# A two-layer attention kernel: the second layer's heads ordered by time, and the last head's row halves exchanged

## The chip, the cores and the metric

The kernel runs on one core of one Trainium2 chip. The metric is the device time of one execution in microseconds, the median of several runs; lower is better. The kernel before takes 1461.78 us (median of 3 runs, 1460.41 to 1463.3).

## The reference

A decoder trunk of two layers on an input of 1024 rows and 1024 columns, in float32. Layer A is differential attention with 8 heads; the change leaves its arithmetic and its order rule alone. Layer B is stick-breaking attention with 16 heads of 64 columns, on keys and values that are projected from layer A's output. Cut to what matters, layer B is

```python
k, v = split(rms(x, kv_norm) @ w_kv)
q, g = split(rms(x, b_norm) @ w_in)
for each head and each block of 128 rows i:
    z = (q_i @ k.T) / 8                          # columns 0 .. (i+1)*128
    log_1mb = where(mask, log_sigmoid(-z), 0)
    suffix = cumsum from the right of log_1mb, without the own column
    a = where(mask, exp(log_sigmoid(z) + suffix), 0)
    o_i = a @ v
x = x + (o * silu(g)) @ w_out
```

The causal mask makes the work of row block i (0 to 7) grow with i + 1: rows 512 to 1023 hold 26/36 of it, rows 0 to 511 hold 10/36.

## The kernel before, in words

Every float32 product is made of three float32r matmuls (high by high, low by high, high by low; two where the weights' low part is left out). Layer B works on 8 pairs of heads. For each pair there are four projections (k, v, q and the gate g), each in two halves of 512 rows, 24 matmuls of 128x512 each (`group`, L195 to L197). They don't depend on the attention of the pair before, and serve as **fill**: while TensorE works on a pair's attention it is given the next pair's projections in between. There are k tiles (`kh`, `kl`) for two pairs only.

The attention of a pair is cut into four **units** m = 0 to 3 of two row blocks, 2m and 2m + 1. A unit has two parts:

- S (`unit_s_b`): the scores of a block (`scores`, L237, one or two chunks of up to 512 columns, matmuls on 64 rows of the array, both heads side by side in PSUM tile `sc`, of which there is one), their copy by ScalarE (L781), the mask by GpSimd (L783), and then the chain: L790 (VectorE), L791 and L792 (ScalarE), L793 and the scan L795 (VectorE), L796 (ScalarE). Blocks 4 to 7 have a tile `zl` for each of the two heads; blocks 0 to 3 have one for both.
- T (`unit_t_b`): for each 256 columns of each head, transposes of the chain's result (`transposed`, L265, into PSUM tile `tr`), their split into `th` (ScalarE, L271) and `tl` (VectorE, L272), three buffers each, and the products with v (L811, L812).

`run_layer` sets the order in which these steps are written: S of one unit, T of the unit before, and so on, in the order 1, 3, 0, 2 (`ORDERS[2]`); `merge` mixes that list with the fill by estimated cost. The list is the order of priority. A scheduler that comes with the language then places each instruction on its engine's queue, and each engine runs its queue in that order.

The last pair has the output projection as its fill (`OutProj`). `last_order` is (1, 0, 3, 2) in the kernel before: the units of rows 0 to 511 first, mixed with the part of their output projection that needs heads 0 to 11 alone; then the units of rows 512 to 1023, mixed with the rest of the output projection of rows 0 to 511; and last, with nothing beside it, the output projection of rows 512 to 1023. The line that picks it is

```python
f0 = last_order[0] // 2
```

Of the kernel before, what the change touches and what calls it, by code (L numbers as in the profile page):

```python
# [19 lines left out]
P = 128  # L20
# [15 lines left out]
def build(tc, ins, out):  # L36
# [9 lines left out]
         "al": 6, "bl": 7, "tb": 3, "oa": 0, "la": 0, "lb": 8, "lt": 0, "lead": 1.0, "leada": 0.02, "leadb": 0.02, "leadxa": 0.15, "leadxb": 0.1, "holda": 0, "holdb": 0, "c2": 1, "gca": 0, "gcb": 0, "prea": 2, "preb": 1, "warm": 16, "wp": 2, "hpx": -1, "nx": 1, "nk": 6, "hpo": 0, "ob": 2, "late": 400}  # L46
# [37 lines left out]
    def zat(n):  # L84
        return zt()
# [97 lines left out]
    def group(n, pairs, done):  # L183
# [3 lines left out]
        size = 4 if n > 256 else 8  # L187
# [39 lines left out]
    def scores(q, k, i, evac):  # L227
# [3 lines left out]
        for off, w in reversed(chunks(n)):  # L231
# [7 lines left out]
            evac(off, w, n, pts)  # L239

# [33 lines left out]

    def v_rows(pt):
        vt = g2k()
        with hp():
            act.activation(vt, pt, AF.Copy)
        tr = PS("tr", B["tr"])
        for r in range(4):  # L280
            pe.transpose(tr[:, r * P:(r + 1) * P], vt[:, r * P:(r + 1) * P], ident)
        return tr


    def merge(main, fill, lead=0.0):
# [4 lines left out]
        while i < len(main) or j < len(fill):  # L290
# [4 lines left out]
            else:  # L295
                df += fill[j][0]
                fill[j][1]()
                j += 1

# [141 lines left out]
    def run_layer(hds, qkv, unit_s, unit_t, xT, og, op, hfs):  # L441
# [66 lines left out]
        for h in range(n - 1):  # L508
            main = []
# [12 lines left out]
        ss = unit_s(h, ma)  # L522
        main = (late + ss if B["lt"] else ss + late) + [(0.0, lambda: gate_mul(hds[h - 1], h - 1, og)),
# [72 lines left out]
    def unit_s_a(h, m):  # L596
        hd = heads_a[h]

        def s_step(qb):
            if hd.o is None:  # L600
                hd.o = [T("o", [P, HALF], B["o"]) for _ in range(2)]
                hd.at = {}
            n = (qb + 1) * P
            p = [zat(n + P), zat(n + P)]
            mn = [small(2), small(2)]

            def evac(off, w, n, pts):
                k = 0 if off == 0 else 1
                mask = mask_a[:, HALF - w:] if off + w == n else mask_a[:, 0:1].to_broadcast([P, w])
                for c in range(2):  # L610
                    dve.tensor_tensor_reduce(p[c][:, off:off + w], pts[:, c, :w], mask, 1.0, BIG, ALU.add, ALU.min,  # L611
                                             mn[c][:, k:k + 1])

            scores(hd.q[qb // 4], hd.k, qb, evac)
            s = small(2)
            for c in range(2):
                b = mn[c][:, 0:1]
                if n > 512:
                    dve.tensor_tensor(b, b, mn[c][:, 1:2], ALU.min)
                act.activation(p[c][:, :n], p[c][:, :n], AF.Exp, bias=b, scale=-1.0, accum_out=s[:, c:c + 1])  # L620
            r = small(2)
            dve.reciprocal(r, s)
            dve.tensor_tensor(r[:, 1:2], r[:, 1:2], nlam, ALU.mult)
            dve.tensor_scalar(p[0][:, :n], p[0][:, :n], r[:, 0:1], None, ALU.mult)
            dve.scalar_tensor_tensor(p[1][:, :n], p[1][:, :n], r[:, 1:2], p[0][:, :n], ALU.mult, ALU.add)
            hd.at[qb] = p[1]

        return [(4 * (qb + 1) * P * 0.42, lambda qb=qb: s_step(qb)) for qb in (2 * m, 2 * m + 1)]

    def unit_t_a(h, m):  # L630
# [3 lines left out]
        def t_step(t):  # L634
# [3 lines left out]
            for i, (kb, th, tl) in enumerate(transposed(hd.at[2 * m], hd.at[2 * m + 1], t, t == m)):  # L638
# [14 lines left out]
        return [(4 * 55 + 6 * 109 + (430 if t == m else 0), lambda t=t: t_step(t)) for t in range(m + 1)]  # L653
# [109 lines left out]
    def unit_s_b(p, m):  # L763
        hd = heads_b[p]

        def s_step(qb):
            if hd.o is None:
                hd.o = [T("o", [P, HALF], B["o"]) for _ in range(2)]
                hd.at = {}
            n = (qb + 1) * P  # L770
            heads = ((0, 1),) if n <= HALF else ((0,), (1,))
            z = [zbt() for _ in heads]
            w2 = len(heads[0]) * n
            for t in z:
                pool.memset(t[:, w2:w2 + 1], 0.0)
# [10 lines left out]
            scores(hd.q[qb // 4], hd.k, qb, evac)  # L786
            for t in z:
                zc = t[:, :w2]
                u = u4k()[:, :w2]
# [92 lines left out]
```

## Time and profile before

| | |
|---|---|
| median of 3 runs | 1461.78 us (1460.41 to 1463.3) |
| the profiled execution | 1463.71 us |
| its span, first to last instruction | 1461.8 us |
| mean granted clock | 0.985 |
| TensorE, matmuls busy | 1409.5 us, 96% |
| VectorE busy | 1073.2 us, 73% |
| ScalarE busy | 927.8 us, 63% |
| GpSimd busy | 294.9 us, 20% |

The busy share of TensorE is the union of its matmuls' spans. Matmuls overlap, so a long row of them is "busy" at any spacing; the idle time between them is a lower bound of what TensorE loses, and the spacing of their starts tells the rest. The first layer's attention runs from about 30 to 570 us, the change of layers to 755 us, the first seven pairs of layer B to 1297 us, the last pair to 1398 us, and what is left of the output projection to the end.

### The profile page before, as it was taken

The numbers are of one execution on the slowest core, as the hardware profiler recorded it, in microseconds if no ns is written. First come the engines' busy times: TensorE is split into PE (matmuls) and PEld (weight loads), VectorE is DVE, ScalarE is ACT, GpSimd is POOL, SyncE is SP. The second block draws the span as 40 slices with busy tenths as digits, with TensorE's granted clock in tenths as the row PEclk, the third lists the DMA queues.
The fourth block names the chain that finished last, engine by engine and source line by source line (L and its number), as shares of the span: only waits on it lengthen the run. The fifth ranks groups of instructions, "written<-read, shape, count | busy, mean of one in ns | idle before, by whom it ended". The sixth has DMA issues, their size and how long they took to land.

```text
span 1461.8 us, 24434 instructions
## 1 busy us (share of the span) xinstructions
PE 1409.5 (96%) x8944; PEld 1188.5 (81%) x8944; DVE 1073.2 (73%) x2219; ACT 927.8 (63%) x1908; POOL 294.9 (20%) x545
## 2 busy tenths in 40 slices
PE   8999999999999999999999999998999999987899
PEld 7888888888888888789877777776778677776699
DVE  7576667677777776775547888878878888888952
ACT  7555556566565655442557777778777877787720
POOL 0111212121212121100011222223233232335100
PEclk9999999999999999999999999999999999998999
DMA  5111111111111115621310011110011010233512
GB/s 203 59 30 44 45 44 44 44 44 44 44 44 44 44 61 185 214 90 58 116 58 29 30 58 29 44 44 30 34 45 38 30 58 30 70 133 111 193 73 80
DMA packets 43111, 99.39 MB, mean 68 GB/s; under 512 B 4848, under 2 KB 6640, under 8 KB 41968
## 3 DMA queue, kind: packets, MB, share of 16 engines
q1 hardware_dynamic: 42992, 97.83, 19.5%
q8 instruction: 71, 1.16, 0.3%
q14 instruction: 48, 0.39, 0.1%
HBM read 74.74 MB, written 23.07 MB: 67 GB/s over the span
## 4 chain that ended last, share of the span: by engine, by line
PE 75%; DVE 12%; ACT 6%; issue 4%; DMA 2%; POOL 1%; SPq 0%; DVEq 0%; POOLq 0%; ACTq 0%
PE proj L195 18%; PE proj L196 17%; PE proj L197 17%; PE sc L237 8%; PE tr L265 5%; DVE u4k L795 4%; DVE u4k L793 2%; DVE tl L272 2%; PE av L811 2%; PE av L812 2%; PE av L642 1%; ACT u4k L791 1%; PE av L640 1%; PE av L641 1%; ACT u4k L792 1%
## 5 line engine op out<-in xcount | busy, mean ns | idle before, releaser
L195 PE MATMUL proj<-ah,w 128*128 128x512 f32 x768 | 309.0, 402 | 5.4 <-DVE kl L245 5.3
L196 PE MATMUL proj<-al,w 128*128 128x512 f32 x768 | 308.5, 402 | 0.0
L197 PE MATMUL proj<-ah,w 128*128 128x512 f32 x768 | 306.4, 399 | 0.0
L195 PE MATMUL proj<-w,ah 128*128 128x256 f32 x992 | 291.2, 294 | 5.2 <-DVE kl L424 2.7
L197 PE MATMUL proj<-w,al 128*128 128x256 f32 x992 | 285.4, 288 | 0.0
L196 PE MATMUL proj<-w,ah 128*128 128x256 f32 x992 | 285.2, 288 | 0.0
L195 PEld LDWEIGHTS proj<-w,ah 128*128 128x128 f32 x992 | 192.3, 194 | 15.6 <-DVE kl L424 4.2
L197 PEld LDWEIGHTS proj<-w,al 128*128 128x128 f32 x992 | 192.3, 194 | 1.9 <-issue 1.6
L196 PEld LDWEIGHTS proj<-w,ah 128*128 128x128 f32 x992 | 192.3, 194 | 1.9 <-issue 1.3
L195 PEld LDWEIGHTS proj<-ah,w 128*128 128x128 f32 x768 | 145.6, 190 | 41.4 <-DVE kl L245 6.6
L795 DVE TENSOR_TENSOR_SCAN u4k<-zl,u4k 128x768 f32<-128x768 f32 (+4 forms) x96 | 173.7, 1812 | 1.0
L196 PEld LDWEIGHTS proj<-al,w 128*128 128x128 f32 x768 | 145.7, 190 | 33.0 <-issue 6.4
L197 PEld LDWEIGHTS proj<-ah,w 128*128 128x128 f32 x768 | 145.7, 190 | 32.1 <-issue 4.2
L237 PE MATMUL sc<-kh,q 64*128 64x512 f32 (+2 forms) x768 | 158.2, 400 | 12.6 <-ACT zl L781 9.8
L272 DVE TENSOR_TENSOR tl<-tr,th 128x512 fp32r<-128x512 f32 (+1 forms) x240 | 145.2, 629 | 32.5 <-ACT th L271 30.6
L783 POOL TENSOR_SCALAR_AFFINE_SELECT zl<-zl 128x128 f32<-128x128 f32 (+1 forms) x96 | 81.8, 857 | 306.3 <-ACT zl L781 298.5
L271 ACT ACTIVATE th<-tr 128x512 fp32r<-128x512 f32 (+1 forms) x240 | 124.4, 553 | 28.8 <-PE tr L265 24.5
L796 ACT ACTIVATE zl<-u4k 128x768 f32<-128x768 f32 (+4 forms) x96 | 81.3, 846 | 93.8 <-DVE u4k L795 81.2
L164 ACT ACTIVATE w<-raw,cols 128x256 fp32r<-128x256 f32 x240 | 104.6, 500 | 45.8 <-PE proj L196 33.5
L265 PE MATMUL tr<-ident,zl 128*128 128x128 f32 x864 | 129.0, 277 | 3.6 <-ACT zl L796 2.0
L611 DVE CUSTOM_DVE_ANT_0 zl<-sc,mask_a 128x384 f32<-128x384 f32 (+3 forms) x192 | 99.0, 552 | 40.7 <-PE sc L237 40.5
L237 PEld LDWEIGHTS sc<-kh,q 64*128 64x128 f32 x768 | 76.0, 187 | 64.6 <-issue 17.5
(146 smaller groups left out, 2590.9 us busy)
## 6 DMA issues: line engine op xcount, KB each, us to landing
raw<-in_w_kv_dram SPq DMA_DIRECT2D x32, 256.0 KB, 2.7
raw<-in_w_b_dram SPq DMA_DIRECT2D x32, 256.0 KB, 2.7
raw<-in_w_qk_dram SPq DMA_DIRECT2D x28, 256.0 KB, 2.7
raw<-in_w_vg_dram SPq DMA_DIRECT2D x28, 256.0 KB, 2.7
og_a<-o SPq DMA_DIRECT2D x28, 256.0 KB, 2.0
og_b<-o SPq DMA_DIRECT2D x28, 256.0 KB, 2.0
raw<-in_a_w_out_dram SPq DMA_DIRECT2D x26, 256.0 KB, 2.9
raw<-in_b_w_out_dram SPq DMA_DIRECT2D x26, 256.0 KB, 2.9
```

Source lines behind the costliest of these rows:

```text
L164: act.activation(h[:, i], r, AF.Copy, scale=g)
L195: pe.matmul(box["p"], lh, rh, start=(j == 0), stop=False)
L196: pe.matmul(box["p"], lh, rl, start=False, stop=False)
L197: pe.matmul(box["p"], ll, rh, start=False, stop=last)
L237: pe.matmul(pts[:, c, :wm], q[a][HI[c], rs_], k[b][HI[c], off:off + wm], start=(a + b == 0), stop=(a == 1))
L265: pe.transpose(pt[:, o:o + P], a[:, (2 * t + b) * P:(2 * t + b + 1) * P], ident)
L271: act.activation(th[:, skip:], pt[:, skip:], AF.Copy)
L272: dve.tensor_tensor(tl[:, skip:], pt[:, skip:], f32(th[:, skip:]), ALU.subtract)
L611: dve.tensor_tensor_reduce(p[c][:, off:off + w], pts[:, c, :w], mask, 1.0, BIG, ALU.add, ALU.min, mn[c][:, k:k + 1])
L783: pool.affine_select(t3[:, :, n - P:], t3[:, :, n - P:], [[0, len(cs)], [-1, P]], ALU.is_ge, -BIG, base=-1, channel_multiplier=1)
L795: dve.tensor_tensor_scan(ur, t[:, 1:w2 + 1][:, ::-1], ur, 0.0, ALU.add, ALU.subtract)
L796: act.activation(zc, u, AF.Exp, scale=-1.0)
```

## The change

1. `B["ob"]` goes from 2 to 10: layer B's units come in the order 2, 3, 1, 0.
2. `B["lb"]` goes from 8 to 4: the last pair's order is (3, 2, 1, 0), so that `f0` is 1. The two halves of rows change places in all that `OutProj` does; the output projection of rows 0 to 511 comes last.
3. For the first seven pairs of layer B, `merge` is replaced by `by_time`. Each step gets a time between 0 and 1 of its pair: the S steps in proportion to their cost; the T steps of a unit from 0.1 after its last S step on, or from the end of the T steps before, spread so that a pair's T steps take 0.9 in all; the fill in proportion to its cost. Steps are written in order of this time, and those past 1 go into the next pair's list.
4. S steps are single chunks of scores and no more whole blocks; T steps are split into the transposes with their copies (`tr_step`) and the products (`av_step`), and `ahead` puts each transpose step ahead of the product step before it. This holds for both layers.
5. The fill's steps in layer B hold 2 instead of 4 groups of three matmuls.
6. In the last pair the T steps that are carried over count 400 each in `merge`.

No instruction is added or removed: TensorE has 8896 matmuls in both programs, and VectorE, ScalarE, GpSimd and the DMA queue have the same counts and shapes.

```diff
-         ... "lb": 8, ... "ob": 2, "late": 400}
+         ... "lb": 4, ... "ob": 10, "late": 400, "lag": 0.1, "pace": 0.9}
-        size = 4 if n > 256 else 8
+        size = (2 if layer[1] else 4) if n > 256 else 8
...
+    def ahead(pairs):
+        r = []
+        for i, (ct, tr, cv, av) in enumerate(pairs):
+            r.append((ct, tr))
+            if i:
+                r.append(pairs[i - 1][2:])
+        return r + [pairs[-1][2:]]
...
+    def by_time(unit_s, unit_t, h, order, fill, carry, gate):
+        units = [(m, unit_s(h, m)) for m in order]
+        total = sum(c for _, ss in units for c, _ in ss)
+        tf = sum(c for c, _ in fill)
+        ev = [(t - 1.0, st) for t, st in carry]
+        if gate:
+            ev.append((carry[-1][0] - 1.0 + 0.02, gate))
+        at, free = 0.0, (carry[-1][0] - 1.0 if carry else 0.0)
+        per = sum(len(unit_t(h, m)) for m in order)
+        for m, ss in units:
+            for c, st in ss:
+                ev.append((at, st))
+                at += c / total
+            t = max(at + B["lag"], free)
+            for _, st in unit_t(h, m):
+                ev.append((t, st))
+                t += B["pace"] / per
+            free = t
+        at = 0.0
+        for c, st in fill:
+            ev.append((at, st))
+            at += c / tf
+        ev.sort(key=lambda e: e[0])
+        for t, st in ev:
+            if t < 1.0:
+                st()
+        return [e for e in ev if e[0] >= 1.0]
...
+            if layer[1]:
+                late = by_time(unit_s, unit_t, h, order, fill(h + 1), late, (lambda h=h: gate_mul(hds[h - 1], h - 1, og)) if h else None)
+                steps, hold = [], 0
+                continue
...
+        if layer[1]:
+            late = [(400.0, st) for _, st in late]
...
-        return [(4 * 55 + 4 * 109, lambda c=c, t=t: t_step(c, t)) for c in range(2) for t in range(m + 1)]
+        return ahead([(4 * 109, lambda c=c, t=t: tr_step(c, t), 4 * 120, lambda c=c, t=t: av_step(c, t))
+                      for c in range(2) for t in range(m + 1)])
```

Two places of TensorE's order. In the rows, `sc` is written by score matmuls, `tr` by transposes of `zl`, `av` by the products and `proj` by the fill; the numbers are buffers. The first place is the boundary of the third and the fourth pair. Before, the scores of block 5 of unit 2 (`sc_11544`) stand there as the last of their pair, and the next pair's `sc_11636` follows:

```order
L237 MATMUL sc_11544<-kh_10031,q_1898_10549 128x512 x2
L237 MATMUL sc_11544<-kl_10032,q_1898_10549 128x512 x2
L237 MATMUL sc_11544<-kh_10031,q_1899_10550 128x512 x2
L265 MATMUL tr_11716<-ident,zl_11464 128x128
L265 MATMUL tr_11747<-ident,zl_11464 128x128
L811 MATMUL av_11580<-th_11585,v_10029 128x256
L812 MATMUL av_11580<-tl_11586,v_10029 128x256
L811 MATMUL av_11580<-th_11585,v_10029 128x256
L812 MATMUL av_11580<-tl_11586,v_10029 128x256
L237 MATMUL sc_11636<-kh_10887,q_2025_11321 128x384 x2
```

With the change the pair's last scores are those of unit 0 (`sc_11529`), and the next pair's first two chunks (`sc_11579` and `sc_11654`, block 4) follow:

```order
L237 MATMUL sc_11529<-kh_9992,q_1880_10435 128x256 x2
L889 MATMUL av_11460<-th_11515,v_9991 128x256
L890 MATMUL av_11460<-tl_11516,v_9991 128x256
L889 MATMUL av_11460<-th_11515,v_9991 128x256
L890 MATMUL av_11460<-tl_11516,v_9991 128x256
L281 MATMUL tr_11683<-ident,zl_11005 128x128
L281 MATMUL tr_11683<-ident,zl_11227 128x128
L281 MATMUL tr_11683<-ident,zl_11005 128x128
L281 MATMUL tr_11683<-ident,zl_11227 128x128
L237 MATMUL sc_11579<-kh_10848,q_2030_11366 128x256 x2
L237 MATMUL sc_11579<-kl_10849,q_2030_11366 128x256 x2
L237 MATMUL sc_11579<-kh_10848,q_2031_11367 128x256 x2
```

The big block has moved away from the boundary, and small chunks of scores stand closer together there, with transposes and products and no projections between them.

The second place is the last pair's last scores. Before, they are block 5's (`sc_15775`), and projections (`proj`) stand among what follows:

```order
L237 MATMUL sc_15775<-kh_14340,q_2643_15004 128x512 x2
L195 MATMUL proj_15994<-q_2730_15537,ah_14932 128x512
L196 MATMUL proj_15994<-q_2731_15538,ah_14932 128x512
L195 MATMUL proj_16002<-q_2730_15537,ah_14932 128x512
L196 MATMUL proj_16002<-q_2731_15538,ah_14932 128x512
L812 MATMUL av_15798<-tl_15831,v_14339 128x256
```

With the change they are block 0's (`sc_15884`), and its first transposes (of `zl_15882`) come after 14 transposes and 20 products without a projection:

```order
L237 MATMUL sc_15884<-kh_14272,q_2598_14727 128x256 x2
L281 MATMUL tr_15902<-ident,zl_15818 128x128
L889 MATMUL av_15476<-th_15500,v_14270 128x256
L890 MATMUL av_15476<-tl_15501,v_14270 128x256
L889 MATMUL av_15476<-th_15500,v_14270 128x256
L890 MATMUL av_15476<-tl_15501,v_14270 128x256
L889 MATMUL av_15476<-th_15515,v_14270 128x256
L890 MATMUL av_15476<-tl_15516,v_14270 128x256
```

The end of the attention now consists of small blocks, and the projections that stood among it have moved behind it.

## Rows read from the trace of the kernel before

**Rows 1.** The page, part 1: busy time, share of the span and instructions.

```profile
PE 1409.5 (96%) x8944; PEld 1188.5 (81%) x8944; DVE 1073.2 (73%) x2219; ACT 927.8 (63%) x1908; POOL 294.9 (20%) x545
```

**Rows 2.** Busy time by stage, with the columns in the first line.

```profile
core 0: us, PE busy (x) PEld busy (x) DVE busy (x) ACT busy (x) POOL busy (x), PEclk, DMA share, GB/s
755.00:1297.00 542.00, 524.36 (x2885) 411.81 (x2883) 445.48 (x608) 422.47 (x768) 152.97 (x296) 0.99 0.14 47
1297.00:1398.00 101.00, 81.36 (x553) 69.58 (x554) 90.48 (x127) 76.23 (x134) 30.97 (x58) 0.92 0.36 123
```

**Rows 3.** Waits of the matmuls, 755 to 1297 us: total us, times, longest.

```profile
PE proj L195 <- DVE kl L245: 5.3, 4, 2.3
PE av L812 <- DVE tl L272: 4.2, 8, 1.8
PE sc L237 <- ACT zl L781: 2.4, 4, 0.9
PE av L811 <- ACT th L271: 2.1, 2, 1.1
PE tr L265 <- ACT zl L796: 1.7, 2, 1.3
PE av L811 <- DVE o L818: 1.2, 2, 0.7
```

**Rows 4.** Busy time in stretches around drops of the clock, columns as in rows 2.

```profile
913.00:918.00 5.00, 4.20 (x11) 3.31 (x12) 3.79 (x7) 3.75 (x6) 0.00 (x0) 0.66 0.01 2
995.00:1004.00 9.00, 7.95 (x27) 6.08 (x26) 7.58 (x11) 6.68 (x10) 0.41 (x1) 0.62 0.01 2
1155.00:1161.00 6.00, 4.71 (x16) 3.23 (x17) 5.44 (x7) 5.13 (x8) 0.72 (x4) 0.72 0.00 0
1309.00:1318.00 9.00, 7.26 (x36) 6.10 (x36) 7.76 (x11) 7.08 (x11) 4.79 (x3) 0.62 0.08 32
1333.00:1342.00 9.00, 6.03 (x31) 5.20 (x33) 8.97 (x15) 7.34 (x15) 4.78 (x4) 0.62 0.57 171
```

**Rows 5.** Matmuls in order of time, 1004.45 to 1005.92: start us, length us.

```profile
1004.45 0.51 PE L237 MATMUL sc<-kh,q 64*128 64x512 f32 x2
1004.78 0.40 PE L237 MATMUL sc<-kl,q 64*128 64x512 f32 x2
1005.02 0.40 PE L237 MATMUL sc<-kh,q 64*128 64x512 f32 x2
1005.35 0.50 PE L195 MATMUL proj<-ah,w 128*128 128x512 f32 x1
1005.68 0.40 PE L196 MATMUL proj<-al,w 128*128 128x512 f32 x1
1005.92 0.40 PE L197 MATMUL proj<-ah,w 128*128 128x512 f32 x1
```

**Rows 6.** Groups of instructions by shape: busy us, mean ns, idle before.

```profile
L790 DVE TENSOR_SCALAR u4k<-zl 128x768 int32<-128x768 int32 x24 | 16.4, 696 | 1.7 <-POOL zl L783 1.4 <-ACT zl L781 0.3
L791 ACT ACTIVATE u4k<-u4k 128x768 f32<-128x768 f32 x24 | 20.0, 837 | 2.0 <-DVE u4k L790 1.9
L792 ACT ACTIVATE u4k<-u4k 128x768 f32<-128x768 f32 x24 | 19.6, 836 | 0.2
L793 DVE SCALAR_TENSOR_TENSOR u4k<-zl,u4k 128x768 f32<-128x768 f32 x24 | 22.9, 969 | 12.4 <-ACT u4k L792 12.4
L795 DVE TENSOR_TENSOR_SCAN u4k<-zl,u4k 128x768 f32<-128x768 f32 x24 | 42.2, 1771 | 0.3
L796 ACT ACTIVATE zl<-u4k 128x768 f32<-128x768 f32 x24 | 20.3, 846 | 18.6 <-DVE u4k L795 18.5
```

**Rows 7.** Waits of the matmuls, 1297 to 1398 us.

```profile
PE sc L237 <- ACT zl L781: 7.4, 3, 4.0
PE av L811 <- DVE o L818: 4.6, 3, 1.9
PE av L812 <- DVE tl L272: 3.0, 5, 1.4
```

More of the change, by code (lines that the diff above doesn't have):

```diff
@@ L230, in scores, with chunk @@
         rs_ = slice((i % 4) * P, (i % 4) * P + P)
-        for off, w in reversed(chunks(n)):
+        def chunk(off, w):
             n_t[0] += 1
@@ L239, in scores, with row_steps, step @@
             evac(off, w, n, pts)
+        return [(4 * w * 0.42, lambda off=off, w=w: chunk(off, w)) for off, w in reversed(chunks(n))]
+    def row_steps(qk, qb, begin, evac, end):
+        def step(j):
+            if j == 0:
+                box["s"] = scores(*qk(), qb, evac)
+                begin()
+            box["s"][j][1]()
+            if j == len(costs) - 1:
+                end()
+        box = {}
+        costs = [4 * w * 0.42 for _, w in reversed(chunks((qb + 1) * P))]
+        return [(c, lambda j=j: step(j)) for j, c in enumerate(costs)]
     def split_rows(h, l, pt, scale):
@@ L597, in unit_s_a, with row, begin @@
         hd = heads_a[h]
[L599 to L602, printed above, removed]
+        def row(qb):
             n = (qb + 1) * P
[L604 to L605 removed]
+            st = {}
+            def begin():
+                if hd.o is None:
+                    hd.o = [T("o", [P, HALF], B["o"]) for _ in range(2)]
+                    hd.at = {}
+                st["p"] = [zat(n + P), zat(n + P)]
+                st["mn"] = [small(2), small(2)]
             def evac(off, w, n, pts):
@@ L610, in evac, with end @@
                 for c in range(2):
[L611 to L628, printed above, removed]
+                    dve.tensor_tensor_reduce(st["p"][c][:, off:off + w], pts[:, c, :w], mask, 1.0, BIG, ALU.add, ALU.min,
+                                             st["mn"][c][:, k:k + 1])
+            def end():
+                p, mn = st["p"], st["mn"]
+                s = small(2)
+                for c in range(2):
+                    b = mn[c][:, 0:1]
+                    if n > 512:
+                        dve.tensor_tensor(b, b, mn[c][:, 1:2], ALU.min)
+                    act.activation(p[c][:, :n], p[c][:, :n], AF.Exp, bias=b, scale=-1.0, accum_out=s[:, c:c + 1])
+                r = small(2)
+                dve.reciprocal(r, s)
+                dve.tensor_tensor(r[:, 1:2], r[:, 1:2], nlam, ALU.mult)
+                dve.tensor_scalar(p[0][:, :n], p[0][:, :n], r[:, 0:1], None, ALU.mult)
+                dve.scalar_tensor_tensor(p[1][:, :n], p[1][:, :n], r[:, 1:2], p[0][:, :n], ALU.mult, ALU.add)
+                hd.at[qb] = p[1]
+            return row_steps(lambda: (hd.q[qb // 4], hd.k), qb, begin, evac, end)
+        return [st for qb in (2 * m, 2 * m + 1) for st in row(qb)]
     def unit_t_a(h, m):
```

59 lines of the change are left out of this document (33 added, 26 removed).

## The prediction

> **What bounds the kernel now.** Read first the busy shares of the whole span [rows 1]: the matmuls are busy for 96% of it, VectorE for 73%, ScalarE for 63%. TensorE is the bound, and its work is the same in both programs, so the change can give back only what TensorE loses. Read next where it loses [rows 2]. In the seven pairs of layer B, 755 to 1297 us, the matmuls leave 542.0 - 524.4 = 17.6 us idle, and VectorE is busy for 82%. In the last pair they leave 101.0 - 81.4 = 19.6 us idle, with VectorE at 90%: there it is nearly the bound, and scores wait for their copy (7.4 us), products for their PSUM tile (4.6) and for `tl` (3.0) [rows 7]. The first layer isn't in these rows; its order changes only by finer steps, and I count it at nothing: its chain is shorter, and its projections, which are still placed beside it, hide it. Without them it would cost as much as layer B's idle time, some 15 us.
>
> Then what ends the waits of the seven pairs [rows 3]. Two kinds stand there. One is the long way of a block: products that wait for `tl` (4.2 us) or `th` (2.1), transposes that wait for the last step of the chain (1.7), 8.0 us in all. The other belongs to the boundary of two pairs: projections that wait for the low part of k (5.3 us), scores that wait until the copy before has emptied the one `sc` tile (2.4), products that wait for their PSUM tile (1.2), 8.9 us in all.
>
> Third, the clock [rows 4]. It stands at full speed but for short drops. A mean of 0.66 over 5 us, 0.62 over 9 us and 0.72 over 6 us make 3.4 + 6.8 + 3.4 = 13.6 us at 1.2 instead of 2.4 GHz in the seven pairs, which costs at most 6.8 us. Each drop lies at a boundary at which TensorE has just waited. In the last pair the mean of 0.92 [rows 2] makes 16 us at 1.2 GHz, at most 8 us lost.
>
> Last, what the profile doesn't count as idle: at 1004.45 to 1005.92 [rows 5] score matmuls start 0.24 us apart, and projections too, but the first pair of scores takes 0.33, the step from scores to projections 0.33 and the first projection 0.33. Entering and leaving a stretch of scores costs 3 x 0.09 = 0.27 us.
>
> **The change part by part.**
>
> *Stretches of scores.* By count of the order, layer B's score matmuls stand in 116 stretches before and in 102 with the change. 14 x 0.27 us = **-3.8 us**. Bounds: 0 (if the gaps are there for another reason) and -5.
> The Trainium skill (TensorEngine Tiling, Key Properties) says that a change of the tiling mode, and not of the tile alone, drains TensorE; it gives no time for that. By that rule alone the finer steps of parts 3 to 5 speak against the change, since each cut of a block of scores or of a fill step can add a change of mode. If the cuts had doubled the 116 stretches, the sum would have 116 x 0.27 = 31 us more. The order decides against this reading here: it has fewer.
>
> *The long way of a block.* The last unit of a pair before is unit 2, and in every second pair (the third, fifth and seventh) its block 5 has little behind it: in the third pair, 21 projections, 8 products and 12 score matmuls stand between its last scores and the first transposition of its result, some 21 x 0.24 + 8 x 0.12 + 12 x 0.15 = 7.8 us (a product has half the columns of a projection; 0.15 is a sixth of the 0.90 us that the scores of rows 5 take). The six steps of the chain for a tile of 768 columns sum to 0.70 + 0.84 + 0.84 + 0.97 + 1.77 + 0.85 = 6.0 us [rows 6], and the second head's steps share VectorE and ScalarE with it: another 0.70 + 0.97 + 1.77 = 3.4 us of VectorE, so 6.0 to 9.4 us, and the copy and the mask come before. 7.8 is too little. With the change the pair ends with units 1 and 0; of the big blocks the one with the least behind it, block 5 of the third pair, has 37 projections, 8 products and 12 score matmuls, 37 x 0.24 + 1.0 + 1.8 = 11.7 us. That covers the chain. The products come later behind their transposes, too. Of the 8.0 us I take back three quarters: **-6 us**. Bounds: 0 and -8.
>
> *The boundary.* k has tiles for two pairs, so the projection of the next k but one waits for the pair's last scores in both kernels, and a stretch of some 6 us without projections stays, as the first place of the order shows. With the change the scores there are closer together: at the third boundary four chunks start within 5.4 us of matmuls, before three within 3. On ScalarE, in order, the copies of `th`, steps of the chain and the two copies of k stand between the copies of these scores. A chunk of scores can't start before the last copy. Against that, the chain that runs there is a small block's, so VectorE reaches the low part of k sooner. Bounds: -5.3 (all waits for k go) and +7.2 (the wait for the copy, 2.4 us, four times as long). I take **+2 us**, nearer to the waits' present size.
>
> *The clock.* With shorter waits one of the four drops of 3.4 us should go: **-1.7 us**. Bounds: 0 and -6.8.
>
> *The last pair.* Units 3 and 2 come first, so the long chains start early; the small blocks come last, and their own chain is short. But by count of the order 192 projections of 256 columns stand between the pair's first scores and its last product, and 253 before: 61 x 0.12 = 7.3 us of cover have moved behind the attention. VectorE's work in that stretch is the same and fills 90% of it. At the second place of the order nothing but transposes and products covers block 0's chain. What is late there is VectorE, and behind it the gate of rows 0 to 511, on which the last projections of these rows wait. Bounds: +7.3 (all the lost cover is waited for) and -8 (the waits stay, and the drops of the clock go). I take **+3 us**. The DMAs move with it: the loads of `OutProj` for each half are issued behind the same stores on SP's queue as before, with the halves exchanged, so I cost them at nothing; what hides them is some 30 us of projections, and if that cover were gone, a late load would stop TensorE for its whole landing.
>
> *The end.* The output projection of rows 0 to 511 has the same size as that of rows 512 to 1023. Nothing changes: 0.
>
> Sum: -3.8 - 6 + 2 - 1.7 + 3 = -6.5 us. The profiled execution took 1463.71 us, 1.9 us more than its span and 1.9 us more than the median of 1461.78. Against the median: 1461.8 - 6.5 = 1455.3, so **1455 us**.
>
> **The rivals.**
>
> *The boundary eats the gain (no change).* For it speaks that the third, fifth and seventh pair have the same stretch without projections in both orders, and that ScalarE must do more between two copies of scores there. Then the boundary costs +7 instead of +2, and the wait brings the drop of the clock back: -6.5 + 5 + 1.7 = +0.2, 1462 us. Against it: the wait for the copy is only 2.4 us now.
>
> *The last pair becomes bound by VectorE (slower).* The place is the stretch from the last scores of unit 2 to the last product. It decides from the point at which VectorE has no idle time left: it has 101 - 90.5 = 10.5 us, most of it while it waits for TensorE and ScalarE in turn. If the 7.3 us of cover are waited for and two more drops of the clock follow (3.4 us), and of the seven pairs only the stretches of scores come back, the sum is -3.8 + 2 + 7.3 + 3.4 = +8.9, say 1470 us; with a part of the long way gained, 1467.
>
> *The seven pairs run without waits (faster by more).* All of rows 3 goes, with the drops of the clock: -3.8 - 16.9 - 6.8 + 3 = -24.5, 1437 us. Against it: the boundary's stretch is still in the order.
>
> *The change doesn't do what it says.* The scheduler and not the list places the instructions. The order shows the units moved, so only a part is open: the projections still come in alternately long and short pairs, which an order by time was to even out.
>
> **How the numbers follow.** My forecast, a gain of 3 to 12 us, gets 0.5; the larger gain 0.06; no change 0.18; the slower case 0.26. The range has to hold most of the first, the third and the likely part of the slower case: from 1443 (the forecast with the full 8 us of the long way, the other three drops of the clock, 5.1 us, and no loss at the boundary or in the last pair: -6.5 - 2 - 5.1 - 5 = -18.6) to 1468 (the slower case with a part of the long way gained). A measurement of this kernel can tell a difference of about 0.2%, 2.9 us. Faster by more than that: 0.55; within: 0.19; slower: 0.26.
>
> **What would show each step.** The waits of the seven pairs: products on `tl` and `th` and transposes on the chain down from 8.0 to about 2 us; scores on their copy up from 2.4. The projections' wait for the low part of k tells whether the boundary got better or worse. Idle time of the matmuls from 755 us to the last pair: 17.6 to about 13. In the last pair: 19.6 to about 22, with VectorE's share above 90%. The clock: three drops or fewer in the seven pairs. The forecast is wrong if scores wait for their copy by more than 10 us, if the idle time of the last pair passes 27 us, or if the first layer, where I expect nothing, moves by more than 2 us.

## The result: slower by 1.4%, and the profile after

The changed kernel takes 1483.3 us (median of 4 runs, 1478.2 to 1486.3) beside 1462.1 for the kernel before in the same runs; the ratio is 1.0142, with a 95% interval of 1.0112 to 1.0173. The forecast was 1455 us, a gain. The profiled execution took 1482.28 us with a span of 1480.4, against 1463.71 and 1461.8 before.

The page of the changed kernel, busy time, beside [rows 1]:

```profile
PE 1413.8 (95%) x8944; PEld 1194.2 (81%) x8944; DVE 1080.1 (73%) x2219; ACT 929.6 (63%) x1908; POOL 293.2 (20%) x545
```

The work of TensorE is the same; the time in which no matmul ran grew from 1461.8 - 1409.5 = 52.3 us to 1480.4 - 1413.8 = 66.6. To see where, I lay the two executions side by side at equal work: each matmul counts by its kind's spacing in a dense row (0.23 us for 512 columns of a projection, 0.12 for 256, 0.14 for 512 columns of scores), and I ask when each kernel had done the same amount. When the kernel before stood at the time in the first line, the other was behind it by (us, minus is ahead):

| the kernel before at | 455 | 556 | 602 | 755 | 1293 | 1408 to the end |
|---|---|---|---|---|---|---|
| the change | -0.7 | 2.9 | 11.7 | 10.5 | 11.7 | 18.6 |
| its layer A in whole steps, old costs | 0.1 | 0.1 | -3.4 | -5.0 | -4.8 | 1.0 |
| its layer A in split steps, old costs | -1.3 | -1.5 | -3.9 | -3.5 | 2.2 | 13.0 |
| before, layer A's new cost alone | 2.5 | 4.4 | 13.0 | 12.2 | 16.8 | 13.5 |
| before, layer A's cost lowered | 5.1 | 5.6 | 4.4 | 2.8 | 10.0 | 5.7 |
| before, last pair's halves exchanged alone | -1.2 | -1.2 | -1.4 | -1.9 | -2.0 | 3.6 |
| the fastest, below | 0.7 | 0.7 | -2.8 | -3.2 | -3.6 | -6.2 |

How far to trust such a table: up to 732 us the kernel before, the change with layer A in whole steps, the exchange alone and the fastest have the same order of instructions on TensorE, VectorE and ScalarE, and still these executions stand up to 5 us apart at 755 us. The profiled execution of the kernel before took 3 us more than that kernel's medians below; it has a wait of 1.7 us at 574 us and a drop of the clock behind it, which some others of the same order lack. So 5 us in one column can be the execution; what changes along a line tells more. The medians below leave out two executions, of 2676 and 3265 us, that lie far outside the rest of their kernels.

The first line is the result in short: about 11 us are lost at the end of layer A, where I expected nothing; nothing is gained in the seven pairs; 7 us are lost in the last pair. The stages of the change, by windows with the columns of [rows 2]; the second and third line are the seven pairs and the last pair, which lie 11 to 12 us later now:

```profile
550.00:600.00 50.00, 41.93 (x281) 33.75 (x279) 36.40 (x107) 27.54 (x62) 8.01 (x12) 0.93 0.35 116
...
766.00:1309.00 543.00, 520.51 (x2886) 413.90 (x2887) 447.81 (x603) 428.36 (x775) 156.49 (x295) 0.98 0.14 46
1309.00:1416.00 107.00, 85.12 (x551) 73.72 (x550) 95.46 (x131) 75.14 (x130) 25.75 (x61) 0.86 0.35 119
```

The first of these in the kernel before, the same view:

```profile
550.00:600.00 50.00, 48.27 (x331) 42.02 (x331) 34.64 (x92) 26.02 (x58) 8.99 (x14) 0.97 0.45 163
```

In these 50 us 281 matmuls started instead of 331, and 8.1 us stood idle instead of 1.7. What the matmuls of the change waited for in that window (total us, times, longest):

```profile
PE sc L237 <- DVE small L675: 3.2, 3, 1.9
PE tr L634 <- POOL qk L629: 2.2, 1, 2.2
PE proj L195 <- DVE g2k L213: 1.0, 1, 1.0
```

The scores of layer A wait until VectorE has emptied the one `sc` tile (L675, which copies and takes the minimum in one pass). Two stretches of the timeline show one such wait. TensorE (start us, length us, instruction, idle before and its releaser):

```profile
572.08 0.39 PE L237 MATMUL sc<-kh,q 64*128 64x512 f32 x2
574.38 0.59 PE L237 MATMUL sc<-kh,q 64*128 64x512 f32 x2 [1.90 <-DVE small L675]
...
578.06 1.33 PE L634 MATMUL tr<-ident,qk 128*128 128x128 f32 x5 [2.24 <-POOL qk L629]
```

VectorE at that time:

```profile
571.38 1.01 DVE L690 SCALAR_TENSOR_TENSOR zl<-zl,small,zl 128x768 f32<-128x768 f32 x1
...
573.02 0.68 DVE L675 CUSTOM_DVE_ANT_0 zl<-sc,mask_a 128x512 f32<-128x512 f32 x1
...
573.63 0.69 DVE L675 CUSTOM_DVE_ANT_0 zl<-sc,mask_a 128x512 f32<-128x512 f32 x1
...
574.24 1.22 DVE L618 TENSOR_TENSOR qk<-qk,small 128x1024 f32<-128x1024 f32 x1
```

The scores of 572.08 are followed by other scores, which need the same tile, and no projection stands between. VectorE, with 1.0 us of the chain (L690) and 0.7 us of small steps ahead of it, gets to the tile's two halves at 573.02, and the next scores start at 574.38. What is missing is cover: projections that TensorE could run meanwhile. The next experiments ask where they went.

### The profile page after: what moved, and what is told of

Read it like the earlier page. It is cut to its first block, busy times and chain, and to the rows that moved or that the text cites. A ratio compares the mean times of both kernels' runs of the same rounds, so it can differ in the third digit from the quotient of the medians.

```text
span 1480.4 us, 24358 instructions
## 1 busy us (share of the span) xinstructions
PE 1413.8 (95%) x8944; PEld 1194.2 (81%) x8944; DVE 1080.1 (73%) x2219; ACT 929.6 (63%) x1908; POOL 293.2 (20%) x545
## 4 chain that ended last, share of the span: by engine, by line
PE 67%; DVE 18%; ACT 8%; issue 4%; DMA 2%; POOL 1%; SPq 0%; DVEq 0%; ACTq 0%; POOLq 0%
PE proj L195 16%; PE proj L196 15%; PE proj L197 15%; DVE u4k L868 7%; PE sc L237 6%; PE tr L281 4%; DVE u4k L866 3%; DVE tl L288 2%; ACT u4k L864 2%; DVE w L165 2%; PE av L890 1%; DVE u4k L863 1%; ACT u4k L865 1%; PE av L712 1%; PE av L889 1%
## 5 line engine op out<-in xcount | busy, mean ns | idle before, releaser
L237 PE MATMUL sc<-kh,q 64*128 64x512 f32 (+2 forms) x768 | 158.0, 399 | 16.4 <-ACT zl L854 10.6
L287 ACT ACTIVATE th<-tr 128x512 fp32r<-128x512 f32 (+1 forms) x240 | 128.4, 551 | 40.6 <-PE tr L281 32.8
L281 PE MATMUL tr<-ident,zl 128*128 128x128 f32 x864 | 140.5, 284 | 6.6 <-DVE tl L288 5.3
L165 DVE SCALAR_TENSOR_TENSOR w<-raw,cols,w 128x256 fp32r<-128x256 f32 x240 | 118.2, 541 | 27.6 <-ACT w L164 26.6
L685 ACT ACTIVATE zl<-zl,small 128x256 f32<-128x256 f32 (+7 forms) x128 | 98.4, 771 | 56.0 <-DVE small L684 40.6
```

The source lines that it names most:

```text
L165: dve.scalar_tensor_tensor(l[:, i], r, g, f32(h[:, i]), ALU.mult, ALU.subtract)
L237: pe.matmul(pts[:, c, :wm], q[a][HI[c], rs_], k[b][HI[c], off:off + wm], start=(a + b == 0), stop=(a == 1))
L281: pe.transpose(pt[:, o:o + P], a[:, (2 * t + b) * P:(2 * t + b + 1) * P], ident)
L287: act.activation(th[:, skip:], pt[:, skip:], AF.Copy)
```

## The experiments

All times are medians of 4 to 10 executions; the kernel before took 1460.3 to 1460.7 us beside them. Ratios are to it, with their 95% intervals.

### Layer A's steps and the last pair's order

Layer A's steps whole again (scores of a block in one step, transposes and products in one step at the old costs), the rest as changed:

```diff
-        return [st for qb in (2 * m, 2 * m + 1) for st in row(qb)]
+        return [(4 * (qb + 1) * P * 0.42, lambda qb=qb: whole(qb)) for qb in (2 * m, 2 * m + 1)]
...
-        return ahead([(4 * 109, lambda t=t: tr_step(t), 6 * 120 + (430 if t == m else 0), lambda t=t: av_step(t)) for t in range(m + 1)])
+        return [(4 * 55 + 6 * 109 + (430 if t == m else 0), lambda t=t: t_step(t)) for t in range(m + 1)]
```

> The change with layer A's steps whole again (one step for a block's scores, one for transposes and products together, the old costs); all else as changed. Theory T1: the 11 us that the traces differ by at the end of layer A (540 to 600 us) come from the finer steps of layer A, so the time falls from 1483 to about 1472 us, and the idle time of the matmuls from 550 to 600 us falls by some 6 us. Rival R1: the loss there comes from what layer B's new list does to the scheduler's placement of the change of layers (fill of layer B's first pair), and layer A's steps don't matter: 1483 us.

Measured: 1466.5 us, ratio 1.0041 (1.0027 to 1.0056). T1 holds, and by more than the 11 us: 17 us lie in these two edits. The idle time from 550 to 600 us went from 8.1 us to none:

```profile
550.00:600.00 50.00, 50.00 (x357) 43.70 (x356) 38.14 (x97) 27.70 (x61) 10.27 (x15) 1.00 0.50 176
```

The last pair's old order (`"lb": 8`), the rest as changed:

> The change with the last pair's old order of units (1, 0, 3, 2), so that rows 512 to 1023 are projected last again; all else as changed. Theory T2: the exchange of the halves costs the 6.5 us by which the last pair falls behind: 1476 to 1477 us. Rival R2: the last pair is late because of its finer steps or because of what the pair before it carries over into it, not of the exchange: 1483 us, the same.

Measured: 1480.2 us, 1.0128 (1.0111 to 1.0145). Only 3 us, too near to the spread of these runs (4 us and more) to choose.

Both edits together:

> Both of the two edits together: layer A's steps whole, and the last pair's old order; what is left of the change is the order by time, the finer steps of layer B and the unit order 2, 3, 1, 0. T1 and T2 with an order by time that gains and loses nothing in the seven pairs: 1465 to 1466 us, within 4 us of the kernel before. If the order by time gains what I had predicted for it (9.5 us without the last pair): 1453 us. R1 and R2: 1483 us.

Measured: 1461.9 us, 1.0006 (0.9996 to 1.0017). So the exchange costs 1466.5 - 1461.9 = 4.6 us here, and what is left of the change (order by time, finer steps of layer B and its fill, units 2, 3, 1, 0) gains nothing.

The exchange alone, in the kernel before (`"lb": 4`):

> The kernel before with the exchange of the last pair's halves alone. T2: 1468 us, 6 us slower than before. R2 (the exchange costs nothing by itself): 1462 us. A third reading, that the exchange gains when the rest is left alone, because the long chains start first: below 1459 us.

Measured: 1465.2 us, 1.0032 (1.0022 to 1.0043), 4.8 us more than before. R2 falls, and T2 holds with a somewhat lower price.

### Which part of layer A's edit

Transposes and products whole, at the old costs; scores in single chunks:

> The change with layer A's transposes and products in one step again, at the old costs; layer A's scores stay in single chunks; all else as changed. The first runs put 17 us on layer A's finer steps (1483 to 1466.5 us). Theory T3: the transposes that go ahead of the products cost it, because with them the scores of the last two heads come late and bunched while VectorE has each of them to empty: 1467 us. Rival R3: the single chunks of scores cost it (each can be put off by itself): 1483 us. If both have a share, between.

Measured: 1467.1 us, 1.0046 (1.0029 to 1.0063). Scores whole; transposes and products split:

> The change with a whole block's scores of layer A in one step again; its transposes and products stay split, with the transposes ahead and the new costs. T3: 1483 us, no gain. R3: 1467 us.

Measured: 1484.6 us, 1.0159 (1.0142 to 1.0177). R3 falls: the single chunks of scores cost nothing, all of it lies in the line of the transposes and products. The traces say why: with the chunks single or whole, TensorE's order is the same but for four matmuls at 99 us. That line changes two things, the steps and their costs. The steps split, with costs that sum to the old ones:

```diff
-        return ahead([(4 * 109, lambda t=t: tr_step(t), 6 * 120 + ...
+        return ahead([(4 * 55, lambda t=t: tr_step(t), 6 * 109 + ...
```

> The change with layer A's steps as fine as changed, but with costs that sum to the old ones (220 for the transposes and 654 for the products, where it has 436 and 720), so that a head's fill is shared out between scores and the rest as before. Rival R4: it is the share of the fill and not the fineness of the steps that puts the scores late: 1467 us. T3 and R3: 1483 us.

Measured: 1475.9 us, 1.0103 (1.0088 to 1.0118): between the two. The split steps with the new costs, but no transposes written ahead:

```diff
-        return ahead([(4 * 109, ...), 6 * 120 + ..., ...) for t in range(m + 1)])
+        return [st for t in range(m + 1) for st in ((4 * 109, lambda t=t: tr_step(t)), (6 * 120 + (430 if t == m else 0), lambda t=t: av_step(t)))]
```

> The change with layer A's transposes and products as separate steps at the changed costs, but each product step written right behind its own transposes, none ahead. T7: the order in which they are written (the transposes ahead) makes up the 9.4 us that are left with the old costs: 1474 us. Rival R7: it is the number of steps, not their order: 1483 us. If both this and the costs are needed for any loss: 1467 us.

Measured: 1483.4 us, 1.0155 (1.0137 to 1.0173). At the new costs the transposes ahead make no difference, so T3, which blamed them, falls there; whether they have a part in the 9.4 us that the split steps cost at the old costs (1475.9 against 1466.5) wasn't tried. And whole steps with the new cost:

> The change with layer A's steps whole, as in the run of 1466.5 us, but with the changed cost of a step of transposes and products (1156 instead of 874, and 430 more for a unit's last, as before). Theory T5: the cost by itself lets the projections run ahead of the scores in layer A, whatever the size of the steps, and that was worth 7.4 us (1483.3 to 1475.9): 1474 us, and the matmuls idle at the end of layer A. Rival R6: the cost matters only where the transposes can go ahead of their products: 1467 us.

Measured: 1480.9 us, 1.0139 (1.0122 to 1.0157). So T5 holds, and with twice its price: the cost of a step, 874 against 1156, takes 14.4 of the 17 us with the steps whole. The two edits don't add: the split alone costs 9.4 us, the new cost alone 14.4, both 16.8. The decisive runs change that one number in the kernel before and nothing else:

```diff
-        return [(4 * 55 + 6 * 109 + (430 if t == m else 0), lambda t=t: t_step(t)) for t in range(m + 1)]
+        return [(4 * 109 + 6 * 120 + (430 if t == m else 0), lambda t=t: t_step(t)) for t in range(m + 1)]
```

> The kernel before with one number changed: a step of transposes and products of layer A counts 1156 instead of 874 (and 430 more for a unit's last step, as before). Theory T5, as it stands after the last runs: this cost by itself lets the projections run ahead of the scores in layer A and takes 14 of the 17 us: 1473 to 1476 us, 10 us or more of it between 530 and 600 us. Rival R10: the cost does this only together with the finer scores of layer B's first pair or the smaller fill steps: 1461 us.

Measured: 1476.7 us, 1.0110 (1.0090 to 1.0130), 16.3 us slower by one number. In the profiled execution 12.2 us of 13.5 are lost before 755 us (the line "new cost alone" of the table), or 14 to 17 against the three others of the table that have the order of the kernel before up to 732 us. How it comes about is read from the score matmuls alone (L237), by stretches of layer A; the columns are the window, its length, the matmuls' busy time and, in brackets, their number, then the same of the weight loads, the clock and the DMA. The kernel before:

```profile
150.00:300.00 150.00, 21.86 (x148) 11.82 (x148) 1.00 0.13 43
300.00:455.00 155.00, 21.17 (x150) 11.89 (x150) 1.00 0.13 42
455.00:550.00 95.00, 14.20 (x102) 7.97 (x102) 1.00 0.19 62
550.00:650.00 100.00, 14.75 (x90) 8.03 (x90) 0.95 0.46 163
```

The kernel before with the new cost:

```profile
150.00:300.00 150.00, 19.78 (x144) 11.13 (x144) 1.00 0.13 43
300.00:455.00 155.00, 23.11 (x144) 12.23 (x144) 1.00 0.14 44
455.00:550.00 95.00, 14.07 (x92) 7.45 (x90) 1.00 0.22 73
550.00:650.00 100.00, 18.46 (x114) 10.02 (x114) 0.93 0.39 139
```

Up to 550 us TensorE loses little (4.4 us at 556), yet there are fewer scores in every stretch, 4 + 6 + 10 = 20 matmuls of the 72 that a head has; projections run in their place. The bill comes when the projections are used up: 114 instead of 90 scores are left for the last 100 us, with less beside them. How much less can be read from TensorE's order, which the program fixes. From the middle of the seventh head's scores to the first of the eighth head's, the kernel before has 122 projections, with the new cost 18 are left, in the changed kernel 29. The projections' matmuls alone in these two stretches (the first window's count has one more at its edge), the kernel before first:

```profile
535.20:572.40 37.20, 27.14 (x123) 1.00 0.56 202
```

```profile
561.80:585.70 23.90, 2.42 (x18) 0.79 0.30 91
```

What the matmuls wait for from 550 to 600 us, the kernel before first:

```profile
PE proj L195 <- DVE kl L424: 1.7, 1, 1.7
```

and with the new cost:

```profile
PE sc L237 <- DVE small L611: 6.2, 3, 2.9
```

Scores that wait for VectorE's copy are the longest waits of the changed kernel too. The number works through `merge`, which gives each step of a head its share of that head's projections. The scores of a head count 4 x 128 x 36 x 0.42 = 7741; its ten product steps counted 10 x 874 + 4 x 430 = 10460 and now 10 x 1156 + 4 x 430 = 13280. The products' share of the projections goes from 57 to 63%, and scores are written behind more projections. In the list this puts the later units' scores behind at most 2% more of a head's projections, about 1 us; that it ends as a lag of a quarter of a head, with the projections gone before the last head, is measured, and how the scheduler makes it so is not settled. The other direction, 590 for 874 (`4 * 38 + 6 * 73`):

> The kernel before with the same number moved the other way: 590 instead of 874. If the loss grows with the share of the fill that the products get (T5), the scores now come earlier than before, and the projections later; what the end of layer A loses before (a wait of 1.7 us and a short drop of the clock at 575 us) can only shrink: 1457 to 1461 us. Rival R11: the old number stands at an optimum, and scores that come too early wait for VectorE in the middle of the layer: 1465 us or more.

Measured: 1470.4 us, 1.0070 (1.0051 to 1.0088). R11 has the time right: of the three numbers tried, 874 is the best. Its reason isn't seen: from 60 to 455 us no wait of the matmuls is listed, before or here. The loss is spread: 5 us before 455 us (1.7 of them in the first 30), and in the profiled execution 7 us in the seven pairs (2.8 to 10.0 in the table), of whose list not a line is changed; the last pair gives 4 back. The same was seen in the run with split steps and old costs: layer A was on time there (3.5 us ahead of the kernel before at 755 us), and the loss lay in layer B, 5.7 us in the seven pairs and 10.8 in the last, where the kernel with whole steps loses 0.2 and 5.8. Its waits in the seven pairs were

```profile
PE av L890 <- DVE tl L288: 11.6, 6, 2.7
PE sc L237 <- ACT zl L854: 10.2, 5, 5.2
PE av L889 <- ACT th L287: 3.7, 3, 1.6
```

though its list for layer B is that of the run of 1466.5 us. In the order of TensorE these two programs agree from 667 to 995 us, through the rest of the change of layers and the first three pairs, and part in the fourth pair. So the placement of a later part hangs on what went before it. In the seven pairs this went with a loss of 5 to 7 us.

### The exchange of the last pair's halves

Of the exchange alone, the last pair's window and its largest waits (beside [rows 2] and [rows 7]):

```profile
1295.00:1399.00 104.00, 81.32 (x532) 69.51 (x533) 89.09 (x121) 75.82 (x132) 26.50 (x54) 0.85 0.34 119
```

```profile
PE av L812 <- DVE tl L272: 8.2, 6, 5.0
PE sc L237 <- ACT zl L781: 5.5, 6, 2.7
PE tr L265 <- ACT zl L796: 4.6, 2, 4.2
```

The idle time is 22.7 us, 3 more than before; the granted clock is 0.85 where it was 0.92. The order of this run has 281 projections between the pair's first scores and its last product, more than the 253 before. The prediction's price for the exchange was cover that moves behind. So I ran the exchange with the order 2, 3, 1, 0, which leaves only 192 there:

> The kernel before with the last pair in the order 2, 3, 1, 0: the halves of rows exchanged as in the change, but unit 2 ahead of unit 3. By count of the order 192 projections of 256 columns stand between the last pair's first scores and its last product, as in the change; in the run with 3, 2, 1, 0 alone (1465.6 us) there are 281, more than the 253 before. If the cover that is moved behind the attention sets the price (the term of the prediction), this takes 1465.6 + 89 x 0.12 = 1476 us, or half of that: 1471 us. Rival R12: the cover doesn't matter, the chains of units 3 and 2 at the start do: 1466 us, as with 3, 2, 1, 0, or less.

Measured: 1468.0 us, 1.0053 (1.0037 to 1.0068). 89 projections less, 10.7 us of cover, go with 2.8 us more. With the chain's wait:

```profile
PE tr L265 <- ACT zl L796: 6.8, 5, 2.7
PE sc L237 <- ACT zl L781: 4.5, 4, 2.8
```

In both runs the transposes wait for the end of the chain, 4.6 and 6.8 us; in the kernel before, in its last pair:

```profile
PE tr L265 <- ACT zl L796: 0.3, 1, 0.3
```

The time lies between R12 (1466 us or less) and the price by cover (1471 or more), nearer to R12. The two longest waits of the exchange alone, 4.2 and 5.0 us, follow each other from 1343 to 1355 us. There the split of a transposed tile stands behind scans of unit 3 (1024 columns) and unit 2 (640) on VectorE, and TensorE waits for it:

```profile
1348.65 3.36 DVE L795 TENSOR_TENSOR_SCAN u4k<-zl,u4k 128x1024 f32<-128x1024 f32 x1
...
1352.32 1.48 DVE L795 TENSOR_TENSOR_SCAN u4k<-zl,u4k 128x640 f32<-128x640 f32 x1
...
1354.14 1.89 DVE L272 TENSOR_TENSOR tl<-tr,th 128x512 fp32r<-128x512 f32 x3
```

```profile
1354.89 0.58 PE L812 MATMUL av<-tl,v 128*128 128x256 f32 x1 [5.03 <-DVE tl L272]
```

So the likely reason is that the long chains of units 3 and 2 come first and together; no run separates this from the cover and the clock, and how the 4.8 us divide between them stays open.

### The order by time, the order of units, the finer steps

From here on layer A is whole and the last pair in its old order (1461.9 us). With the old order of units 1, 3, 0, 2 in the seven pairs (`"ob": 2`):

> Layer A's steps whole and the last pair's old order (1462.1 us so far), and in the seven pairs the order by time with the old order of units 1, 3, 0, 2. Theory T4: the order of units 2, 3, 1, 0 is what makes the scores stand close together at the boundary and wait for their copy (2.9 us at two of the seven boundaries), and without it the order by time gains some 4 us: 1458 us. Rival R5: the order 2, 3, 1, 0 is what covers the long chain, and without it the waits for the two halves of a transposed tile grow: 1466 us or more.

Measured: 1458.3 us, 0.9979 (0.9970 to 0.9989), 3.6 us less, as T4 has it; R5 falls. Its reason isn't shown by this: the scores' wait for their copy is gone from the head of the list, but at 1297 us the profiled executions of the two kernels stand within 1 us of each other, and 1.6 us of the gain lie in the last pair. Then without the order by time too, by taking the branch out of `run_layer`:

```diff
-            if layer[1]:
-                late = by_time(unit_s, unit_t, h, order, fill(h + 1), late, ...)
-                steps, hold = [], 0
-                continue
```

> The kernel that took 1458.3 us (layer A whole, the old orders of units everywhere) with the order by time taken out of the seven pairs again; what is left of the change is the finer steps of layer B, the fill's smaller steps and the carried steps' count of 400. Theory T9: the order by time gains nothing by itself, since the scheduler places by readiness: 1458 us. Rival R9: it gains the 2.4 us by which that kernel beats the one before, or more: 1461 us or more.

Measured: 1455.4 us, 0.9967 (0.9955 to 0.9980), and a second time, with 5 rounds:

> The best so far once more, for its interval: 1455 us, ratio 0.9967 to the kernel before.

Measured: 1456.6 us, 0.9967 (0.9957 to 0.9978). R9 falls: the order by time gains nothing; that it costs 2 or 3 us isn't certain, since the intervals overlap. This kernel beats both: it is the kernel before with the finer steps of layer B, the fill's steps of 2 groups and the carried steps' count of 400. It also keeps the changed cost of layer B's transposes and products (4 x 109 + 4 x 120 = 916 a step for 656), which `merge` reads again here. Its windows in the seven pairs and in the last:

```profile
752.00:1293.00 541.00, 520.17 (x2884) 409.78 (x2884) 449.25 (x610) 424.47 (x770) 166.70 (x297) 0.99 0.14 47
1293.00:1392.00 99.00, 81.64 (x557) 69.35 (x555) 89.50 (x125) 75.20 (x131) 26.77 (x57) 0.91 0.36 126
```

Against [rows 2] the last pair is 2 us shorter. Up to 769 us its order is that of the kernel before, so its lead of 3 us there is no gain of the program. In the seven pairs more time is idle (20.8 against 17.6 us) and yet none is lost. Which of its parts does it? The fill's smaller steps alone, in the kernel before:

> The kernel before with one part of the change alone, the fill's steps of layer B of 2 instead of 4 groups. In the traces of the runs with layer A whole, 3.4 us come back at about 575 us, where layer B's first projections begin. Theory T8: this comes from the smaller steps: 1457 us. Rival R8: it comes from the rest of the change: 1461 us, the same.

Measured: 1463.0 us, 1.0017 (1.0008 to 1.0026): a loss of 2.4 us, T8 falls. The fastest kernel without them:

> The best so far (1455.4 us: the kernel before with the finer steps in layer B alone, the fill's steps of 2 groups and the carried steps' count of 400) with the fill's steps of 4 groups again. The smaller fill steps alone made the kernel before slower by 2.4 us; if that holds here: 1453 us. If the finer steps of the attention need a finer fill: 1458 us or more.

Measured: 1461.7 us, 1.0005 (0.9994 to 1.0016). So the two kinds of finer steps gain only together: each alone is worth between 0 and a loss of 2.4 us. Whether the fineness of the attention's steps or their new cost has the gain was not tried. Without the count of 400:

> The best so far (1455.4 us) without the count of 400 for the steps that the last pair takes over; what is left of the change is the finer steps of layer B's attention and of its fill. In the traces the best kernel gains 3.2 us at 575 us, nothing in the seven pairs that stays, and 2.6 us in the last pair. Theory T13: the count of 400, which puts the carried products ahead of the fill, gives the gain in the last pair: 1458 us. Rival R13: the finer steps give it: 1455 us.

Measured: 1456.6 us, 0.9971 (0.9960 to 0.9982). T13 falls: the count can do nothing, since `merge` has a lead of 1.0 in the last pair and there writes all of the attention's steps ahead of the fill, whatever they count. The orders of TensorE, VectorE and ScalarE in the two traces are the same, so this is the fastest kernel a third time.

## Why the prediction was wrong, step by step

*The first layer.* This is the step that failed. The text reads "its order changes only by finer steps, and I count it at nothing". The finer steps do cost nothing in layer A itself (with them, at the old costs, it was 3.5 us ahead), though they cost 9.4 us in all, which the profiles put in layer B, where the scheduler's order changed behind them. But the diff also has the line with the new costs, and in layer A `merge` still turns costs into places. That number alone makes the kernel before 16.3 us slower. The cover that I named, the projections "still placed beside it", was what it moved: 18 instead of 122 are left ahead of the last head. My own bound for the loss of that cover, 15 us, comes near, but it was borrowed from layer B's idle time, so that is luck; and I gave the case no chance.

*The long way of a block* (-6 us): wrong in sign. The waits of the seven pairs in the change, beside [rows 3]:

```profile
PE sc L237 <- ACT zl L854: 8.9, 6, 2.9
PE av L890 <- DVE tl L288: 7.7, 6, 2.4
PE av L889 <- ACT th L287: 4.8, 4, 1.7
PE av L889 <- DVE o L896: 0.4, 1, 0.4
PE proj L195 <- DVE kl L261: 0.3, 1, 0.3
```

Transposes no longer wait for the chain, as I had said, but products wait 7.7 + 4.8 us for `tl` and `th` where it was 4.2 + 2.1: in all 12.5 us for 8.0, so +4.5. What is late now is the split of the transposed tile. One of the two longest of these waits, on VectorE's timeline of the change:

```profile
916.80 1.56 DVE L866 SCALAR_TENSOR_TENSOR u4k<-zl,u4k 128x1024 f32<-128x1024 f32 x2
918.28 3.03 DVE L868 TENSOR_TENSOR_SCAN u4k<-zl,u4k 128x1024 f32<-128x1024 f32 x2
921.23 0.53 DVE L288 TENSOR_TENSOR tl<-tr,th 128x384 fp32r<-128x384 f32 x1
```

and the product that waits for it:

```profile
921.90 0.36 PE L890 MATMUL av<-tl,v 128*128 128x256 f32 x1 [2.32 <-DVE tl L288]
```

The scans of two other blocks (1024 and 256 columns), 3.0 us, stand ahead of the split, and TensorE had run out of other work at 919.6. I had counted the matmuls that cover a chain, and not what stands ahead of the split on its engine.

*The boundary* (+2 us): right in kind, and in its sum by luck. Scores wait for their copy 8.9 us instead of 2.4, the projections for the low part of k 0.3 instead of 5.3, the products for their PSUM tile 0.4 instead of 1.2: 9.6 for 8.9, +0.7. Both parts moved as I had named them, but nearly to their bounds, +6.5 of +7.2 and -5.0 of -5.3, and cancel.

*The clock* (-1.7 us): wrong. The mean over 766 to 1309 us fell from 0.99 to 0.98; the drops together are 24 us at 1.2 GHz instead of 13.6, which costs up to 5 us more.

*Stretches of scores* (-3.8 us): not measured by itself, but the rest of the seven pairs, +4.5 + 0.7 and up to 5 for the clock, is 5 to 10 us, and the table shows 1.2. Something gave back 4 to 9 us; the 14 stretches less are a candidate.

*The last pair* (+3 us): mis-sized, and its price had the wrong reason. The idle time is 21.9 us, as forecast ("about 22"), but the clock went from 0.92 to 0.86, and the pair lost 7 us against the kernel before. What it waits for:

```profile
PE av L889 <- DVE o L896: 5.3, 3, 2.8
PE tr L281 <- DVE tl L288: 5.3, 4, 2.7
PE av L890 <- DVE tl L288: 4.7, 2, 4.1
PE proj L195 <- DVE kl L479: 2.2, 1, 2.2
```

VectorE ends each of these. It is busy for 95.46 of 107 us, 89%, so it was late without being full. The exchange alone costs 4.8 us with more cover than before, so the 7.3 us of lost cover that I priced are not what it rests on.

*The end* (0): right. From 1408 us on the difference stays at 18.6 us.

The slower rival (1467 to 1470 us, the last pair bound by VectorE) comes near the change without layer A's two edits, 1466.5 us, but by luck: its last pair loses 5.8 us by the table, where the rival had 7.3 + 3.4. In the changed kernel VectorE ends the waits of the last pair, as the rival has it, without being full. The old costs alone are not enough to come back into the range: with the steps still split the time is 1475.9 us.

## What to carry to other kernels

A cost that a planner reads is part of the program: read a diff for every number that orders work, in every stage that still uses it, and compare the order there too. Here TensorE's order, which is fixed before any run, shows the scores slip behind projections through the first layer.

Work that serves as cover has to last as long as what it covers. A stage that runs ahead on its cover shows nothing in its waits until the cover is used up, so count how much of each kind is left at every boundary and not only who waits.

Where a scheduler places the instructions, a change upstream moves the order downstream. Some 5 us were lost in pairs whose list had not changed, so a small gain is to be tried with more than one neighbour before it is put down to its reason.

## What the runs showed of the hardware

The granted clock costs more in the last pair than I had counted. The exchange alone added 3 us of idle time there, but the mean clock went from 0.92 over 101 us to 0.85 over 104, that is from 16 to 31 us at 1.2 instead of 2.4 GHz. In the 14 us that hold the end of its wait of 4.2 us and the one of 5.0 nearly all is at 1.2 GHz. In the fastest kernel's last pair, with 17.4 us of idle time and a clock of 0.91, a single wait of 2.3 us, which ends at 1303.0, is followed by 10 us at 1.2 GHz:

```profile
1346.00:1360.00 14.00, 7.51 (x35) 7.22 (x36) 13.63 (x17) 7.50 (x13) 4.42 (x8) 0.51 0.77 291
```

```profile
1304.00:1314.00 10.00, 7.62 (x35) 6.45 (x33) 9.70 (x13) 8.26 (x14) 0.41 (x1) 0.50 0.31 105
```

So the length of a wait doesn't tell how long the clock then stays low, and what does is not shown by these runs. The idle time of the last pair alone ranks these kernels rightly (17.4, 19.6, 22.7 us) but sizes the loss too low. In the seven pairs it ranks them wrongly: the fastest kernel has 3 us more of it than the one before, at the same clock, 0.99, and loses no time.
